# Down products of a Strassen feed-forward: operands prepared two pairs of steps ahead instead of one, with three weight tiles loaded before the loop

## The chip, the cores and the metric

The kernel runs on one core of one Trainium2 chip. The time is device microseconds (us) of one launch; the lower the better. The kernel before was timed three times: 1554.86, 1557.81 and 1557.93 us, median 1557.81.

The core's engines work in parallel, each from its own queue in program order, and wait for each other by semaphores: TensorE (PE; PEld is its weight load), VectorE (DVE), ScalarE (ACT), GpSimd (POOL) and SyncE (SP), whose queue issues the DMAs here.

## The reference

One layer of a streaming encoder over 1024 positions of 1024 channels, in float32. Its last part is what the change touches, a gated feed-forward with 2816 inner channels:

```python
h = rmsnorm(x, norm_ffn_w[l])
u = causal_dwconv(h @ w_up[l], conv_ffn_w[l]) + conv_ffn_b[l]
gate, up = jnp.split(u, 2, axis=-1)
x = x + (jax.nn.silu(gate) * up) @ w_down[l]
return rmsnorm(x, norm_final_w)
```

Before it stand an input projection, a gated delta-rule mixer, a banded attention, and an output projection. None of them is touched.

## The kernel before

**Precision.** TensorE multiplies a reduced float32 (F32R). Every operand is therefore split: a high part, made by a cast on ACT, and a low part, the operand minus its high part, made by a subtraction on DVE or POOL. A product is three matmuls: high by high, high by low, low by high.

**Down product.** `silu(gate)*up` is called y: 22 blocks of 128 inner channels. The product of y with `w_down` is done by Strassen's method with seven products of half-size matrices in place of eight. The list `plan` (line 1435) has them in the order P1, P5, P6, P3, P7, P2, P4. Each product has FH = 11 steps of 128 channels, so there are NS = 77 steps, and `down_step(s)` (line 1521) does one: 4 tiles of 128 positions times three matmuls of 128x512, that is 12 matmuls. Products accumulate in two sets of four PSUM tiles (`psd`); when a product ends, `evacuate` adds its sums to the residual `x2` on DVE, up to three a pair of steps.

**Operands of a step.** The left operand is a sum of blocks of y. These sums are formed by `a_sums` on DVE while y is made, and stored to the DRAM tensor `dA`. `a_load(k)` (line 1445) reads the two blocks of the pair k (steps 2k and 2k+1) back into a tile `araw`, of which there are two. `prep_a(k)` (line 1470) makes `ah` (ACT) and `al`: by DVE for odd k in P5, P6, P7 and P4, by POOL otherwise. There are two `ah` and two `al` tiles, the tags "hi" and "lo" of the pool `wst`, which the earlier stages use too. The right operand is a weight block of `w_down` (W11, W12, W22, W21, 11 tiles of 256 KB each) or a difference of two, which `w_sum` writes over a block, on DVE. `prep_w(k)` (line 1486) does the sums for the steps of pair k+1 and then splits the two weight blocks of pair k into `wdh` (ACT) and `wdl` (DVE). These live in five slots, `whs[s % 5]` and `wls[s % 5]`.

**Order.** Everything on DVE, ACT, POOL and SP in this stage is issued through `Pinned` (line 1162; its line 1170 is the one that the profile names), which keeps the program order on each engine. On TensorE the first matmul of each step is kept in order, and a planner places the others.

**Start of the stage.** While the last pair of up products (`r`) is still running, the pool `fr` (line 1591) takes the place of three sums of Strassen's up products, `XT1`, `XT2`, `XT3` (16 KB of high and low part a partition each), and gets W11 and the five slots. The steps 0 to 3 stand between the last pieces of the up stage: loads of W11, `prep_w(0)`, `prep_a(1)`, `prep_w(1)`, steps 0 and 1, `prep_a(2)`, `prep_w(2)`, `a_load(4)`, the last `a_sums` (four DVE operations on `yu` and two stores to `dA`), steps 2 and 3, `prep(3)`. Then the pool `fd` (line 1638) takes the place of the up stage's inputs BH and BL and of its working tiles, and gets W12, W22, W21 and `x2`.

**The loop** (line 1702) goes over the pairs k from 2. In an iteration it issues on SP `a_load(k + 2)` (from k = 3) and those loads of weights and of `x2` that are due, by a list `loads` of (step, tile, source); then `prep(k + 1)` (from k = 3, so that pair 3 is prepared ahead of the loop); then up to three evacuations, up to two steps of the final RMSNorm, and the matmuls of steps 2k and 2k+1. Steps 74 to 76 are done tile by tile after the loop, with the last sums and stores between them; pair 38 is step 76 alone, and its ah and al lie in `fr`.

Of the kernel before, what the change touches and what calls it, by code (L numbers as in the profile page):

```python
# [16 lines left out]
P = 128  # L17
# [29 lines left out]
def hybrid_kernel(ctx: ExitStack, tc: tile.TileContext, a):  # L47
# [1326 lines left out]
    def a_stores(y0, y1, i):  # L1374
        Q.dma_start(dA[0, i], y0[:, h0])
        Q.dma_start(dA[1:3, i].rearrange("s p t -> p s t"), y1.rearrange("p (s t) -> p s t", s=2))
# [65 lines left out]
    def w_src(name, f):  # L1442
        r, c = {"W11": (f, 0), "W12": (f, 1), "W22": (FH + f, 1), "W21": (FH + f, 0)}[name]
        return a["w_down"][r * P:(r + 1) * P, c * HN:(c + 1) * HN]

    def a_load(k):
        raw = wst.tile([P, 2, HN], F32, tag="raw", name="araw")
        for j in range(min(2, NS - 2 * k)):
            pi, f = divmod(2 * k + j, FH)
            Q.dma_start(raw[:, j], dA[plan[pi][1], f])  # L1450
        ring[k] = raw
# [3 lines left out]
    def w_block(s):  # L1455
        q, f = plan[s // FH][0], s % FH
        return {"P1": W11, "P3": W22, "P7": W22, "P2": W21}.get(q, W12)[f]
# [12 lines left out]
    def prep_a(k):  # L1470

        n = min(2, NS - 2 * k)
        raw = ring.pop(k)
        if n == 2:
            ah = wst.tile([P, 2, HN], F32R, tag="hi", name="ah")
            al = wst.tile([P, 2, HN], F32R, tag="lo", name="al")
        else:
            ah = fr.tile([P, 1, HN], F32R, tag="W11_0", name="ah")
            al = fr.tile([P, 1, HN], F32R, tag="W11_1", name="al")
        S.copy(ah[:, 0:n], raw[:, 0:n])  # L1480
        (V if k % 2 and plan[2 * k // FH][0] in ("P5", "P6", "P7", "P4") else G).tensor_tensor(
            out=al[:, 0:n], in0=raw[:, 0:n], in1=ah.bitcast(F32)[:, 0:n], op=ALU.subtract)
        for j in range(n):
            opa[2 * k + j] = (ah, al, j)

    def prep_w(k):

        n = min(2, NS - 2 * k)
        for s in range(2 * k + 2, min(2 * k + 4, NS)):
            if plan[s // FH][0] == "P2":  # L1490
                w_sum(s + FH)
            elif plan[s // FH][0] != "P4":
                w_sum(s)
        for s in range(2 * k, 2 * k + n):
            S.copy(whs[s % 5], w_block(s))
        for s in range(2 * k, 2 * k + n):
            V.tensor_tensor(out=wls[s % 5], in0=w_block(s), in1=whs[s % 5].bitcast(F32), op=ALU.subtract)
            opw[s] = (whs[s % 5], wls[s % 5])

    def prep(k):  # L1500

# [19 lines left out]
    def down_step(s):  # L1521
        pi, f = divmod(s, FH)
        q, ai, ac, first, dest = plan[pi]
        if f == 0 and first:
            acc[ac] = [ps_tile("psd") for _ in range(4)]
        for t in range(4):
            i = down_mm(acc[ac][t], s, t, first and f == 0, f == FH - 1 or (q == "P4" and f == FH - 4),
                        skip_group_check=not first)
            if t == 0:
                tc.keep_in_program_order(i)  # L1530
        if f == FH - 1:
            evac.extend((i, th_, dh, acc[ac][i]) for th_, dh in dest for i in range(4))
# [60 lines left out]
    def fr_tiles(name, dt, r):  # L1593
        return [fr.tile([P, HN], dt, tag=f"{name}{i}", name=f"{name}{i}") for i in r]

    W11 = fr_tiles("W11_", F32, range(5))
    for i in (0, 2):
        whs += fr_tiles("wdh", F32R, range(i, i + 2))
# [6 lines left out]
    a_load(2)  # L1605
    for f in range(5, FH):
        Q.dma_start(W11[f], w_src("W11", f))
    prep_w(0)
    r.sum_pd()
    r.P3()  # L1610
# [12 lines left out]
    p.up_b()  # L1623
    p.mul()
    a_stores(ys[0], p.yu, FH - 1)
    down_step(0)
    down_step(1)
    prep_a(2)
# [7 lines left out]
    fx.close()  # L1636
    bigx.close()
    fd = ctx.enter_context(tc.tile_pool(name="fd", bufs=1, reuse_waits="tile"))
    W12.extend(fd.tile([P, HN], F32, name=f"W12_{f}") for f in range(FH))
    x2 = [fd.tile([P, D], F32, name=f"x2_{t}") for t in range(NT)]  # L1640
    W22.extend(fd.tile([P, HN], F32, name=f"W22_{f}") for f in range(FH))
    W21.extend(fd.tile([P, HN], F32, name=f"W21_{f}") for f in range(FH))
# [2 lines left out]

    loads = []
    for f in range(FH):
        loads.append((3 + f, W12[f], w_src("W12", f)))
        loads.append((15 + f, W22[f], w_src("W22", f)))
        loads.append((34 + f, W21[f], w_src("W21", f)))  # L1650
    for b, s in (((0, 0), 6), ((1, 1), 16), ((0, 1), 27), ((1, 0), 45)):
        for i in range(4):
            t, c = 4 * b[0] + i, slice(b[1] * HN, (b[1] + 1) * HN)
# [47 lines left out]
    TAIL = NS - 3  # L1701
    for k in range(2, (NS + 1) // 2):
        s = 2 * k
        if k > 2 and 2 * (k + 2) < NS:
            a_load(k + 2)
        while loads and loads[0][0] <= s + 1:
            _, d_, s_ = loads.pop(0)
            Q.dma_start(d_, s_)
        if k > 2 and s + 2 < NS - 1:
            prep(k + 1)  # L1710
        if s + 4 == NS - 1:
            prep(k + 2)
        for _ in range(min(3, len(evac))):
            evacuate(*evac.pop(0))
        if s == 5 * FH + 5:
            normed = early_steps()
        if s == 6 * FH:
            normed = norm_steps()
        for _ in range(2):
            next(normed, None)  # L1720
        for j in range(s, min(s + 2, TAIL)):
            down_step(j)
# [96 lines left out]
```

## Time and profile before

| | |
|---|---|
| runs | 1554.86, 1557.81, 1557.93 us |
| profiled execution | 1555.1 us, span of its instructions 1553.3 us |
| PE busy | 1518.1 us (98%), 7687 matmuls |
| PEld busy | 1245.5 us (80%) |
| DVE busy | 1091.1 us (70%) |
| ACT busy | 716.3 us (46%) |
| POOL busy | 639.3 us (41%) |
| TensorE clock granted | 0.998 |
| first matmul of the down products | 1323.3 us from the span's start |
| last one | 1544.7 us |

The span counts from the first to the last instruction; what lies around it is 1.8 us. A matmul's recorded length (0.39 us) is longer than its share of the engine, since matmuls overlap: they follow one another in some 0.22 us. So the number of matmuls in a stretch tells how well PE was fed, better than its busy time does. A row of the timeline has start, length, engine, line, operation, the tiles (out<-in), the shape, the count, and in brackets the idle time ahead of it with what ended it.

### The profile page before, as it was taken

To read this page: it belongs to the slowest core of one execution; us is meant where nothing else is said; L and a number is where in the kernel's file an instruction comes from. 1 tells how busy PE (TensorE), PEld (TensorE's weight loads), DVE (VectorE), ACT (ScalarE), POOL (GpSimd) and SP (SyncE) were. 2 spreads that over 40 slices of the span, in tenths; PEclk is the share of its full clock that TensorE was granted. 3 is DMA by queue.
4 is the path that set the end of the run, shared out by engine and by line. 5 is a ranking of instruction groups with operands and counts; after the bars stand their busy time and mean duration, and the time that the engine had idled before them with its cause. 6 is when DMAs were issued, how large, how long until landed. Compare 5 with 4: busy or idle time off the path is not lost.

```text
span 1553.3 us, 21372 instructions
## 1 busy us (share of the span) xinstructions
PE 1518.1 (98%) x7687; PEld 1245.5 (80%) x7687; DVE 1091.1 (70%) x2146; ACT 716.3 (46%) x1408; POOL 639.3 (41%) x603
## 2 busy tenths in 40 slices
PE   8999999999999999999999999999999999999997
PEld 6878787877778888887887878888888888788875
DVE  7874857948436877866564477777777777786886
ACT  7735536363225656644222255444444443433344
POOL 3633323313132111111221178877777774323253
PEclk9999999999999999999999999999999999999999
DMA  8122121212131101114553223332322333764523
GB/s 300 43 70 65 52 94 45 72 49 92 57 107 50 37 24 58 50 42 153 173 164 109 95 76 108 102 102 102 102 102 102 102 102 113 268 223 161 183 82 142
DMA packets 74506, 162.04 MB, mean 104 GB/s; under 512 B 15648, under 2 KB 16928, under 8 KB 74400
## 3 DMA queue, kind: packets, MB, share of 16 engines
q1 hardware_dynamic: 74400, 160.68, 31.3%
q8 instruction: 60, 0.98, 0.3%
q14 instruction: 46, 0.38, 0.1%
HBM read 120.55 MB, written 40.11 MB: 103 GB/s over the span
## 4 chain that ended last, share of the span: by engine, by line
PE 49%; DVE 3%; issue 2%; DMA 1%; ACT 1%; SPq 1%; POOL 0%; POOLq 0%; DVEq 0%; ACTq 0%
PE psph L52 8%; PE pb L52 7%; PE psd L52 6%; PE psout L52 5%; PE pa L52 5%; PE pc L52 5%; PE pb L1156 4%; PE psd L1511 3%; PE pa L1156 3%; PE pc L1156 2%; DVE wdl L1170 1%; DVE yu L1170 1%; PE pso L52 1%; SPq L1170 1%; DMA araw<-dA 1%
## 5 line engine op out<-in xcount | busy, mean ns | idle before, releaser
L84 POOL TENSOR_TENSOR wlo<-wraw,whi 128x256 fp32r<-128x256 f32 x196 | 157.1, 831 | 442.0 <-ACT whi L81 262.8
L52 PE MATMUL psph<-BH,whi 128*128 128x512 f32 x688 | 280.1, 407 | 8.2 <-ACT BH L225 5.5
L52 PE MATMUL psph<-BL,whi 128*128 128x512 f32 x688 | 275.3, 400 | 0.1
L52 PE MATMUL psph<-BH,wlo 128*128 128x512 f32 x688 | 274.8, 399 | 0.0
L52 PEld LDWEIGHTS psph<-BH,whi 128*128 128x128 f32 x688 | 130.4, 189 | 29.9 <-ACT BH L225 5.5
L1170 POOL TENSOR_TENSOR ol<-wraw,oh 128x512 fp32r<-128x512 f32 x110 | 150.3, 1383 | 6.6 <-ACT oh L1170 6.5
L52 PEld LDWEIGHTS psph<-BL,whi 128*128 128x128 f32 x688 | 130.4, 190 | 22.5 <-DVE BL L226 2.1
L52 PEld LDWEIGHTS psph<-BH,wlo 128*128 128x128 f32 x688 | 130.3, 189 | 22.6
L1170 POOL TENSOR_TENSOR al<-araw,ah 128x1024 fp32r<-128x1024 f32 (+1 forms) x28 | 68.9, 2461 | 145.5 <-ACT ah L1170 145.4
L52 PE MATMUL psd<-wdl,ah 128*128 128x512 f32 (+1 forms) x311 | 121.1, 389 | 5.6 <-DVE wdl L1170 5.6
L52 PE MATMUL psd<-wdh,ah 128*128 128x512 f32 (+1 forms) x311 | 119.5, 387 | 1.5 <-ACT wdh L1170 1.5
L1170 POOL TENSOR_TENSOR wraw<-wraw 128x512 f32<-128x512 f32 x86 | 119.0, 1383 | 4.9
L1511 PE MATMUL psd<-wdh,al 128*128 128x512 f32 (+1 forms) x311 | 120.4, 387 | 0.0
L1170 ACT CAST oh<-wraw 128x512 fp32r<-128x512 f32 x110 | 67.8, 620 | 103.6 <-POOL wraw L1170 103.5
L1170 DVE TENSOR_TENSOR wdl<-W,wdh 128x512 fp32r<-128x512 f32 x77 | 88.9, 1192 | 28.1 <-ACT wdh L1170 28.1
L1170 ACT CAST ah<-araw 128x1024 fp32r<-128x1024 f32 (+1 forms) x39 | 40.6, 1040 | 112.9 <-PE psd L52 50.2
L81 ACT CAST whi<-wraw 128x1024 fp32r<-128x1024 f32 (+2 forms) x61 | 55.3, 907 | 79.3 <-PE psph L52 65.9
L1170 POOL TENSOR_TENSOR gl<-wraw,gh 128x512 fp32r<-128x512 f32 x42 | 56.1, 1337 | 68.9 <-ACT gh L1170 68.9
L52 PEld LDWEIGHTS psd<-wdl,ah 128*128 128x128 f32 x311 | 58.4, 188 | 19.9 <-DVE wdl L1170 8.2
L52 PEld LDWEIGHTS psd<-wdh,ah 128*128 128x128 f32 x311 | 58.4, 188 | 14.0 <-ACT wdh L1170 2.0
L1156 PE MATMUL pa<-BH,gh 128*128 128x512 f32 x176 | 68.6, 389 | 0.0
L52 PE MATMUL pa<-BH,gl 128*128 128x512 f32 x176 | 68.5, 389 | 0.0
(343 smaller groups left out, 3820.4 us busy)
## 6 DMA issues: line engine op xcount, KB each, us to landing
wraw<-w_up SPq DMA_DIRECT2D x44, 512.0 KB, 5.1
wraw<-w_tiles SPq DMA_DIRECT2D x42, 512.0 KB, 3.6
araw<-dA SPq DMA_DIRECT2D x77, 256.0 KB, 3.0
dA<-yu SPq DMA_DIRECT2D x33, 512.0 KB, 3.2
W<-w_down SPq DMA_DIRECT2D x44, 256.0 KB, 4.9
xt<-x SPq DMA_DIRECT2D x16, 512.0 KB, 5.0
dG<-gt SPq DMA_DIRECT2D x16, 512.0 KB, 2.8
ta<-dG SPq DMA_DIRECT2D x16, 256.0 KB, 3.1
```

Of the source, the lines that this page charges most:

```text
L52: last["mm"] = nc.tensor.matmul(*args, **kw).ins
L81: nc.scalar.copy(hi, src)
L84: nc.gpsimd.tensor_tensor(out=lo[:, k:k + 2], in0=src[:, k:k + 2], in1=hi.bitcast(F32)[:, k:k + 2], op=ALU.subtract)
L1156: i = nc.tensor.matmul(ps, wh[:, k], xh[:, k], start=start and k == 0, stop=False, **kw)
L1170: return lambda *args, **kw: tc.keep_in_program_order(f(*args, **kw))
L1511: i = nc.tensor.matmul(ps, al[:, j, ts], wh[:, es], start=False, stop=stop, **kw)
```

## The change

The operands of pair k+2, not of k+1, are prepared in iteration k. For that:

- a third set of `ah` and `al` in the two tiles "gt" of the pool `stg` (they held the gates of the up stage), for every k with k % 3 == 2;
- seven slots for `wdh` and `wdl` instead of five, the new ones in the tiles "p1" and "q" of the up stage;
- the first three W12 tiles in `fr`, ahead of W11, so at the place of XT1, with W11 and the slots moved up by three tiles; they are loaded on SP behind W11, ahead of `prep_w(0)`;
- the loads in the list come earlier: W12 by four steps, W22 and W21 by two;
- `a_load(k + 3)` stands where `a_load(k + 2)` stood, and `a_load(5)` is in the iteration k = 2, behind the loads that are due there (W12 tiles 3 to 6);
- `prep(k + 2)` from k = 2 on, so `prep(4)` follows `prep(3)` directly.

```diff
@@ prep_a
-            ah = wst.tile([P, 2, HN], F32R, tag="hi", name="ah")
-            al = wst.tile([P, 2, HN], F32R, tag="lo", name="al")
+            ah, al = (stg.tile([P, 2, HN], F32R, tag="gt", name=n_) if k % 3 == 2 else
+                      wst.tile([P, 2, HN], F32R, tag=t_, name=n_) for t_, n_ in (("hi", "ah"), ("lo", "al")))
@@ prep_w
-            S.copy(whs[s % 5], w_block(s))
+            S.copy(whs[s % 7], w_block(s))
...
-            V.tensor_tensor(out=wls[s % 5], in0=w_block(s), in1=whs[s % 5].bitcast(F32), op=ALU.subtract)
-            opw[s] = (whs[s % 5], wls[s % 5])
+            V.tensor_tensor(out=wls[s % 7], in0=w_block(s), in1=whs[s % 7].bitcast(F32), op=ALU.subtract)
+            opw[s] = (whs[s % 7], wls[s % 7])
@@ start of the stage
+    W12 += fr_tiles("W12_", F32, range(3))
     W11 = fr_tiles("W11_", F32, range(5))
...
     for f in range(5, FH):
         Q.dma_start(W11[f], w_src("W11", f))
+    for f in range(3):
+        Q.dma_start(W12[f], w_src("W12", f))
     prep_w(0)
...
     a_stores(ys[0], p.yu, FH - 1)
+    for t_ in ("p1", "q"):
+        whs.append(stp.tile([P, HN], F32R, tag=t_, name="wdh", bufs=2))
+        wls.append(stp.tile([P, HN], F32R, tag=t_, name="wdl", bufs=2))
     down_step(0)
...
-    W12.extend(fd.tile([P, HN], F32, name=f"W12_{f}") for f in range(FH))
+    W12.extend(fd.tile([P, HN], F32, name=f"W12_{f}") for f in range(3, FH))
...
-        loads.append((3 + f, W12[f], w_src("W12", f)))
-        loads.append((15 + f, W22[f], w_src("W22", f)))
-        loads.append((34 + f, W21[f], w_src("W21", f)))
+        if f > 2:
+            loads.append((f - 1, W12[f], w_src("W12", f)))
+        loads.append((13 + f, W22[f], w_src("W22", f)))
+        loads.append((32 + f, W21[f], w_src("W21", f)))
@@ the loop over pairs
-        if k > 2 and 2 * (k + 2) < NS:
-            a_load(k + 2)
+        if k > 2 and 2 * (k + 3) < NS:
+            a_load(k + 3)
         while loads and loads[0][0] <= s + 1:
             _, d_, s_ = loads.pop(0)
             Q.dma_start(d_, s_)
-        if k > 2 and s + 2 < NS - 1:
-            prep(k + 1)
-        if s + 4 == NS - 1:
+        if k == 2:
+            a_load(5)
+        if 2 * (k + 2) < NS:
             prep(k + 2)
```

## The prediction

> **What bounds the kernel now.** I read busy time in equal stretches first, then every wait of TensorE's weight loads (PEld) in the stage of the down products, then the other engines around those waits.
>
> ```profile
> 1320.00:1340.00 20.00, 20.00 (x90) 16.55 (x89) 14.99 (x26) 10.75 (x16) 6.73 (x3) 1.00 0.70 244
> 1340.00:1360.00 20.00, 17.86 (x77) 13.81 (x76) 15.76 (x16) 6.27 (x9) 8.00 (x4) 1.00 0.85 296
> ...
> 1400.00:1420.00 20.00, 20.00 (x90) 16.53 (x90) 12.34 (x11) 8.19 (x12) 7.20 (x3) 1.00 0.41 130
> ...
> 1480.00:1500.00 20.00, 18.29 (x81) 14.82 (x81) 18.89 (x20) 9.71 (x16) 11.66 (x6) 1.00 0.33 107
> 1500.00:1520.00 20.00, 20.00 (x89) 16.41 (x90) 14.80 (x15) 9.52 (x17) 7.98 (x5) 1.00 0.25 79
> 1520.00:1540.00 20.00, 16.74 (x72) 13.01 (x71) 15.93 (x19) 8.23 (x14) 7.79 (x5) 1.00 0.40 144
> ```
>
> The columns are: stretch, length, then PE, PEld, DVE, ACT, POOL busy with counts, granted clock, DMA share, GB/s. PE sets the pace (20.00 of 20 in most stretches), at full clock (1.00). A full stretch has 90 matmuls in 20 us, 0.222 us each. Short of 90 are 13 in 1340 to 1360, 9 in 1480 to 1500, 1 in 1500 to 1520 and 18 in 1520 to 1540: 41 matmuls, 9.1 us. That is all that better feeding of PE can give here: 2.9 us early, 6.2 us late (28 matmuls). The waits behind it:
>
> ```profile
> 1343.88 0.19 PEld L52 LDWEIGHTS psd<-wdl,ah 128*128 128x128 f32 x1 [0.85 <-DVE wdl L1170]
> 1346.67 0.19 PEld L52 LDWEIGHTS psd<-wdl,ah 128*128 128x128 f32 x1 [0.88 <-DVE wdl L1170]
> 1356.38 0.19 PEld L52 LDWEIGHTS psd<-wdl,ah 128*128 128x128 f32 x1 [1.67 <-DVE wdl L1170]
> 1499.84 0.19 PEld L52 LDWEIGHTS psd<-wdl,ah 128*128 128x128 f32 x1 [2.14 <-DVE wdl L1170]
> 1528.24 0.19 PEld L52 LDWEIGHTS psd<-wdl,ah 128*128 128x128 f32 x1 [1.27 <-DVE wdl L1170]
> 1536.65 0.19 PEld L52 LDWEIGHTS psd<-wdh,ah 128*128 128x128 f32 x1 [1.96 <-ACT wdh L1170]
> 1538.02 0.19 PEld L52 LDWEIGHTS psd<-wdl,ah 128*128 128x128 f32 x1 [1.19 <-DVE wdl L1170]
> ```
>
> Counting 24 matmuls a pair from the first down product, these are steps 6 and 7 (pair 3), 10 (pair 5), 62 (pair 31), 72 (pair 36) and 76 (pair 38). PE always waits for the split of a weight block, never for the activations.
>
> **The steady rhythm, and what the lead changes.**
>
> ```profile
> 1443.35 1.05 ACT L1170 CAST ah<-araw 128x1024 fp32r<-128x1024 f32 x1 [3.35 <-issue]
> 1448.79 1.05 ACT L1170 CAST ah<-araw 128x1024 fp32r<-128x1024 f32 x1 [3.35 <-PE psd L52]
> 1487.78 3.48 DVE L1170 TENSOR_TENSOR W<-W,W 128x512 f32<-128x512 f32 x2
> 1491.18 1.28 DVE L1170 TENSOR_TENSOR wdl<-W,wdh 128x512 fp32r<-128x512 f32 x2
> 1492.39 1.88 DVE L1170 TENSOR_TENSOR x<-psd,x 128x512 f32<-128x512 f32 x3
> 1494.18 3.92 DVE L1170 TENSOR_TENSOR W<-W,W 128x512 f32<-128x512 f32 x2
> 1498.03 4.55 DVE L1170 TENSOR_TENSOR wdl<-W,wdh 128x512 fp32r<-128x512 f32 x2
> ```
>
> A pair lasts 1448.79 - 1443.35 = 5.44 us. The split ah(k+1) starts when pair k-1 leaves its tile, so a preparation has one pair, 5.44 us, to finish. With three ah/al sets and seven wdh/wdl slots, ah(k+2) waits for the same pair k-1, at the same moment, but is due one pair later: 10.9 us. The raw ring stays at two, and a load k+3 is released by the preparation of k+1 as a load k+2 was by k. So in the steady state no engine gets work or waits added; two products just stand ready.
>
> DVE shows why the lead matters: at 1487.78 a pair needs 3.48 + 1.28 + 1.88 = 6.6 us of DVE against 5.44. Two plain subtractions take 1.28; they take 3.48 with one al on POOL beside them, 2.2 us of waiting, and 4.55 where POOL has more in a row.
>
> **Late waits, one by one.** Steps 62, 63: DVE is behind by the two W sums at 1494.18 and the locked wdl; 2.1 us late against a new slack of 5.44. The W sums of an iteration also move one iteration ahead of the ot products that POOL makes there. Removed. Step 72 is 1.3 us late behind norm work on DVE: removed. Step 76:
>
> ```profile
> 1523.70 2.06 SPq L1170 DMA_DIRECT2D out_dram<-ot  x2
> 1525.87 1.20 SPq L1170 DMA_DIRECT2D araw<-dA  x2
> 1530.08 2.07 SPq L1170 DMA_DIRECT2D out_dram<-ot  x2
> 1532.25 0.37 SPq L1170 DMA_DIRECT2D araw<-dA  x1
> 1535.46 0.62 ACT L1170 CAST ah<-araw 128x512 fp32r<-128x512 f32 x1 [3.45 <-DMA araw<-dA]
> ```
>
> The last load (1532.25) stands on SP behind the stores of ot at 1530.08, and lands at 1535.46. Moved one iteration up it stands behind the stores of 1523.70, that is at about 1525.9, 6.4 us earlier. Both waits of step 76 (1536.65 and 1538.02) go. Late gain: 6.2 us. Bounds: 0 if the lead is eaten up on the way, 6.2 if not. I take 6.2, since even the stretch with DVE at 18.89 is surrounded by 12.34 and 14.80 of 20.
>
> **The early waits** are the real question, because the lead has to be built there.
>
> ```profile
> 1333.29 1.14 ACT L1170 CAST wdh<-W 128x512 fp32r<-128x512 f32 x2
> 1336.96 1.05 ACT L1170 CAST ah<-araw 128x1024 fp32r<-128x1024 f32 x1 [2.52 <-issue]
> 1352.26 1.05 ACT L1170 CAST ah<-araw 128x1024 fp32r<-128x1024 f32 x1 [7.77 <-DMA araw<-dA]
> 1333.47 2.42 POOL L1170 TENSOR_TENSOR al<-araw,ah 128x1024 fp32r<-128x1024 f32 x1 [5.27 <-ACT ah L1170]
> 1338.09 2.40 POOL L1170 TENSOR_TENSOR al<-araw,ah 128x1024 fp32r<-128x1024 f32 x1 [2.20 <-ACT ah L1170]
> 1343.53 2.55 POOL L1170 TENSOR_TENSOR al<-araw,ah 128x1024 fp32r<-128x1024 f32 x1 [3.04 <-ACT ah L1170]
> 1335.77 1.28 DVE L1170 TENSOR_TENSOR wdl<-W,wdh 128x512 fp32r<-128x512 f32 x2
> 1339.02 4.20 DVE L1170 TENSOR_TENSOR yu<-yu 128x512 f32<-128x512 f32 x4 [1.97 <-DMA dA<-yu]
> 1343.14 3.48 DVE L1170 TENSOR_TENSOR wdl<-W,wdh 128x512 fp32r<-128x512 f32 x2
> 1353.86 3.07 DVE L1170 TENSOR_TENSOR wdl<-W,wdh 128x512 fp32r<-128x512 f32 x2 [2.19 <-ACT wdh L1170]
> 1336.34 1.28 SPq L1170 DMA_DIRECT2D araw<-dA  x2
> 1342.52 1.10 SPq L1170 DMA_DIRECT2D dA<-yu  x2
> 1343.71 2.33 SPq L1170 DMA_DIRECT2D W<-w_down  x3
> 1346.61 0.43 SPq L1170 DMA_DIRECT2D araw<-dA  x1
> DMA to landing us min/median/max: 2.6/4.0/5.6
> ```
>
> *Step 6.* ah(3) need no longer wait until 1336.96; it follows the wdh casts, at 1334.4. So al(3) follows al(2) on POOL at about 1336.5 (the first wdl of 1335.77 goes between) to 1338.9, and holds up wdl(5) to 1339.6, just when step 5 needs it. The four sums yu then start at 1339.6 and are not held up (before, the first was, by al(3) at 1338.09). At 0.73 us each, the first three end at 1341.8. But now al(4) comes early too: araw(4), issued by 1337.6, lands 2.6 to 4.0 us on, 1340.2 to 1341.6; from the start of ah to POOL's al are 1.1 us (1336.96 to 1338.09), and POOL holds the port for 2.4 us ahead of the last yu sum or of wdl(6). wdl(6) is ready at about 1345.3, not 1343.8, and wdl(7) at 1346.0, not 1346.6. The two waits become one of about 2.2; pair 3 ends about 0.6 us later than before.
>
> *Step 10.* Before, ah(5) waits for araw(5), which lands at 1352.26, 5.65 us after its second half was issued (1346.61); then al(5) holds POOL and wdl(10) is done only at 1356.4, 4.1 us after the landing. W12_0 was not what ended that wait. The diff puts a load 5 behind four tiles of W12 (3 to 6) instead of three: one more issue, 2.33 / 3 = 0.78 us. The stores before them follow the yu sums: the last one ends at 1342.5 if al(4) comes after it, at 1344.7 if before. Store 0.6, four tiles 3.1, half of araw 0.5, landing 5.65: 1352.3 or 1354.5. wdl(10) is then ready at 1356.4 or 1358.6, against 1356.38 before: 0 to 2.2 us worse, centre 1.0. Because ah(6) now follows at once, al(6) lands between wdl(10) and wdl(11): step 11 waits another 0.3.
>
> The Trainium skill, "DMA: Bandwidth & Descriptors", section "Anatomy of one DMA — SWDGE (gpsimd) path", fits 2.0 us plus bytes at 436 GB/s (for POOL's queue, not SP's): an estimate of 2.6 us for 256 KB. By it araw(5) would land about 3 us sooner, step 10 would hardly wait, and the sum would be near -7; the 5.65 us of this very load decides against it.
>
> The three early loads of W12 cost SP 3 x 0.78 = 2.3 us, in the gap before it may load araw(3); they and the moved W22 and W21 issues (two steps earlier, same count) cost nothing while PE needs none of these for 5 us; uncovered, 0.8 us a tile. The third ah/al set in the gate's tiles and the two slots in the p1 and q tiles cost nothing: their last readers, the last pair's gate and its sum with p1, stand on DVE ahead of the wdl of 1335.77. At worst a cast waits for one of them, 0.7 us as a yu sum.
>
> The 0.6 us of pair 3 goes into the wait of step 10, whose end is set by the load. New early loss: 1.0 + 0.3 = 1.3 us, between -2.9 (all waits go) and +3.5 (2.2, and 1.3 where wdl(11) too meets a whole al of 2.4).
>
> **Sum:** -6.2 + 1.3 = -4.9 us. The profiled execution took 1555.1 us (span 1553.3), the runs 1554.86, 1557.81 and 1557.93: from the profile 1550.2, from the median 1552.9. I give 1552.0, between them. The likeliest case's own range is 1549 to 1554.5.
>
> **Rivals.**
> A, *the lead is whole from the start*: araw(5) lands by about 1350, or al(4) never stands before wdl(6). All 41 matmuls come back: -9.1, from the profile 1546.0, from the median 1548.7. For it: step 10's sum for W12_0 no longer needs a load of that stretch. Against: araw(5) is queued later, not earlier.
> B, *the early stall doubles*: araw(5) lands at about 1356 or later. Early loss +3.5, net -2.7: 1552.4 to 1555.1. For it: DMA is at 0.85 in that stretch. Against: the bytes of three tiles left it.
> C, *slower*: DVE never gets ahead. If the port lock makes a pair cost DVE more than 5.44 us on average from pair 10 to 35, the lead stays nil, the late 6.2 returns, and the early 1.3 to 3.5 is paid: 1556.4 to 1558.6 against 1555.1; past 0.2% from an early loss of 3.1. For it: 6.6 us a pair at 1487.78. Against: 12.34 of 20 in 1400 to 1420.
>
> The Trainium skill, "SBUF — State Buffer", section "Who interferes with whom", says that issue order decides who is blocked, for the whole instruction. It speaks against preparing early: POOL's al issued sooner gets ahead of DVE. The 3.48 us for two wdl at 1343.14 agrees; by it alone the early loss nears case B, by DVE's turn between two POOL instructions (1498.03) it stays near 1.3.
>
> **How the numbers follow.** Forecast 0.55, A 0.17, B 0.13, C 0.15. A measurement of this kernel can tell about 0.2%, 3.1 us, from no change. Forecast and A are faster: 0.72. B and half of C are the same: 0.20. Slower: 0.08. The range 1547 to 1557 leaves out the far ends of A and C.
>
> **What would show it.** Right: no wait of PEld after 1360 on wdl or wdh; the ah casts of the steady state still 5.44 us apart; one wait near 1345 and one near 1357; 90 matmuls in each stretch from 1480 to 1540. Wrong: araw(5) landing before 1350 (A), the wait at step 62 still there (C), or a new wait on W or al in the middle, which I have not priced.

## The result, and the profile after

The changed kernel takes 1549.04 us (median of 6 runs, 1547.27 to 1550.08) against 1556.75 us for the kernel before on the same chip (median of 6): 7.7 us less, ratio 0.9948, 95% interval 0.9938 to 0.9958. The prediction was 1552.0 us with a range of 1547 to 1557. Direction and range were right; the forecast gain of 4.9 us was 2.8 us short.

The profiled execution of the changed kernel took 1549.47 us (span 1547.7). Its stage of down products began 1.65 us later than in the profile of before. Such differences come without the change too: a kernel below that is edited only near the end of the stage ("last load early") began it at 1325.00. So times of two traces are best compared from the stage's first matmul. These are the first and the last matmul of the stage, from the timeline of PE (start, duration, engine, line, operation); first before, then after.

```profile
1323.32 0.39 PE L52 MATMUL psd<-wdh,ah 128*128 128x512 f32 x1
1544.71 0.28 PE L1511 MATMUL psd<-wdh,al 128*128 128x256 f32 x1
```

```profile
1324.97 0.39 PE L52 MATMUL psd<-wdh,ah 128*128 128x512 f32 x1
1539.13 0.28 PE L1511 MATMUL psd<-wdh,al 128*128 128x256 f32 x1
```

The stage took 1544.71 - 1323.32 = 221.4 us before and 1539.13 - 1324.97 = 214.2 us after: 7.2 us less. Busy time in the same equal stretches as in the prediction (PE, PEld, DVE, ACT, POOL with counts, granted clock, DMA share, GB/s), of the changed kernel:

```profile
1340.00:1360.00 20.00, 18.62 (x81) 14.81 (x80) 15.56 (x15) 6.36 (x10) 8.21 (x4) 1.00 0.82 275
...
1480.00:1500.00 20.00, 20.00 (x90) 16.57 (x89) 18.89 (x21) 9.26 (x16) 11.19 (x7) 1.00 0.33 107
1500.00:1520.00 20.00, 20.00 (x90) 16.57 (x89) 14.63 (x14) 11.31 (x20) 9.26 (x5) 1.00 0.27 79
```

The late stretches are full: 90 matmuls where 81 stood. From 1520 to the end PE waits nowhere either. The early stretch has 81 instead of 77. All waits of TensorE's weight loads that are left in the stage:

```profile
1356.90 0.19 PEld L52 LDWEIGHTS psd<-wdl,ah 128*128 128x128 f32 x1 [1.34 <-DVE wdl L1170]
1359.69 0.19 PEld L52 LDWEIGHTS psd<-wdl,ah 128*128 128x128 f32 x1 [0.89 <-DVE wdl L1170]
```

They are steps 10 and 11. The wait near 1345 that the prediction named at step 6 is not there. The other engines around that place, in the changed kernel (start, duration, engine; in brackets the idle time before and what ended it):

```profile
1336.01 1.06 ACT L1170 CAST ah<-araw 128x1024 fp32r<-128x1024 f32 x1
1344.01 1.05 ACT L1170 CAST ah<-araw 128x1024 fp32r<-128x1024 f32 x1 [5.91 <-PE psd L52]
1352.77 1.05 ACT L1170 CAST ah<-araw 128x1024 fp32r<-128x1024 f32 x1 [6.66 <-DMA araw<-dA]
...
1340.85 2.86 DVE L1170 TENSOR_TENSOR yu<-yu 128x512 f32<-128x512 f32 x4
1343.63 1.29 DVE L1170 TENSOR_TENSOR wdl<-W,wdh 128x512 fp32r<-128x512 f32 x2
1354.37 5.27 DVE L1170 TENSOR_TENSOR wdl<-W,wdh 128x512 fp32r<-128x512 f32 x2 [4.24 <-ACT wdh L1170]
...
1335.15 5.23 POOL L1170 TENSOR_TENSOR al<-araw,ah 128x1024 fp32r<-128x1024 f32 x2 [5.28 <-ACT ah L1170]
1345.15 2.63 POOL L1170 TENSOR_TENSOR al<-araw,ah 128x1024 fp32r<-128x1024 f32 x1 [4.77 <-ACT ah L1170]
1353.89 5.20 POOL L1170 TENSOR_TENSOR al<-araw,ah 128x1024 fp32r<-128x1024 f32 x2 [6.12 <-ACT ah L1170]
...
1338.02 1.29 SPq L1170 DMA_DIRECT2D araw<-dA  x2
1343.01 1.10 SPq L1170 DMA_DIRECT2D dA<-yu  x2
1344.20 2.92 SPq L1170 DMA_DIRECT2D W<-w_down  x4
1347.22 1.81 SPq L1170 DMA_DIRECT2D araw<-dA  x4
```

ah(3) came early, at 1336.01, as the prediction said, and al(3) ran behind al(2) (POOL 1335.15, two instructions). But ah(4) came only at 1344.01, so POOL was free from 1340.4 to 1345.15. The four sums yu ran unhindered in 2.86 us (4.20 before), and wdl(6) and wdl(7) took 1.29 us from 1343.63 (3.48 before). That clears steps 6 and 7. At step 10 the picture is the predicted one: ah(5) waits for its load, al(5) and al(6) follow each other on POOL, and the two wdl beside them take 5.27 us.

### The profile page after: what moved, and what is told of

It reads as the page before. It is cut to its first block, busy times and chain, and to the rows that moved or that the text cites. A ratio compares the mean times of both kernels' runs of the same rounds, so it can differ in the third digit from the quotient of the medians.

```text
span 1547.7 us, 21371 instructions
## 1 busy us (share of the span) xinstructions
PE 1517.9 (98%) x7687; PEld 1245.4 (80%) x7687; DVE 1091.1 (70%) x2146; ACT 716.4 (46%) x1408; POOL 640.8 (41%) x603
## 3 DMA queue, kind: packets, MB, share of 16 engines
q1 hardware_dynamic: 74400, 160.68, 31.4%
## 4 chain that ended last, share of the span: by engine, by line
PE 54%; DVE 1%; DMA 1%; issue 0%; ACT 0%; POOL 0%; POOLq 0%; SPq 0%; DVEq 0%; ACTq 0%
PE psd L52 9%; PE psph L52 8%; PE pb L52 8%; PE pa L52 5%; PE psout L52 5%; PE pc L52 5%; PE psd L1511 4%; PE pb L1156 4%; PE pa L1156 3%; PE pc L1156 3%; PE pso L52 1%; PE pst L1044 0%; PE psp L877 0%; DMA tb<-dG 0%; DMA woraw<-w_out 0%
## 5 line engine op out<-in xcount | busy, mean ns | idle before, releaser
L1170 DVE TENSOR_TENSOR wdl<-W,wdh 128x512 fp32r<-128x512 f32 x77 | 95.0, 1272 | 27.6 <-ACT wdh L1170 27.5
L52 PE MATMUL pa<-BL,gh 128*128 128x512 f32 x176 | 68.5, 389 | 0.0
```

The costliest lines, as they stand in the source:

```text
L52: last["mm"] = nc.tensor.matmul(*args, **kw).ins
L1170: return lambda *args, **kw: tc.keep_in_program_order(f(*args, **kw))
```

## The experiments

Eleven kernels were made from the changed one or from the kernel before. Each was timed in five rounds or more beside the kernel before. "Against before" is the difference of the medians of one call. The stage length is worked out from the profile as above.

| kernel | against before, us | ratio, 95% interval | stage, us |
|---|---|---|---|
| before | | | 221.4 |
| changed | -7.7 | 0.9948 (0.9938 to 0.9958) | 214.2 |
| early tiles alone | -0.7 | 0.9996 (0.9987 to 1.0005) | 221.5 |
| lead alone | -5.0 | 0.9963 (0.9950 to 0.9977) | 218.4 |
| araw(5) first | -11.0 | 0.9933 (0.9920 to 0.9945) | 212.2 |
| lead from pair 12 | -9.3 | 0.9943 (0.9931 to 0.9956) | 214.2 |
| last load early | -3.6 | 0.9979 (0.9970 to 0.9988) | 218.7 |
| al(6) on DVE | -8.4 | 0.9942 (0.9928 to 0.9955) | 213.8 |
| araw(4) early | -5.9 | 0.9961 (0.9949 to 0.9973) | 216.2 |
| activations ahead | +1.4 | 1.0007 (0.9998 to 1.0016) | 223.8 |
| activations ahead, late only | -7.3 | 0.9956 (0.9942 to 0.9969) | 217.0 |
| weights ahead | -10.6 | 0.9933 (0.9921 to 0.9946) | 212.6 |
| weights ahead, two sets | -3.7 | 0.9978 (0.9968 to 0.9988) | 218.9 |

**The two parts of the change alone.** The kernel before with the three early W12 tiles and nothing else:

```diff
+    W12 += fr_tiles("W12_", F32, range(3))
...
+    for f in range(3):
+        Q.dma_start(W12[f], w_src("W12", f))
...
-        loads.append((3 + f, W12[f], w_src("W12", f)))
+        if f > 2:
+            loads.append((3 + f, W12[f], w_src("W12", f)))
```

> The kernel before with only the three early W12 tiles; no lead. My theory (the place of araw(5) in the SP queue sets the wait at step 10): araw(5) now stands behind the two stores alone, 3 x 0.78 = 2.3 us earlier, so it lands near 1350 instead of 1352.3 and wdl(10) is done near 1354, before step 10 needs it. The wait of 1.67 at step 10 goes, about 1.4 us; the waits at steps 6 and 7 and the 6.2 us of late waits stay. Total 1.4 us faster than before (0.1%). Rival (the tiles themselves were what PE waited for): the same gain, but araw(5) lands no earlier and the wait of ah(5) on its DMA is as long as before, 7.8 us. Rival (the tiles were hidden anyway): 0.

And the changed kernel without them, all W12 tiles loaded in the loop:

```diff
-    W12 += fr_tiles("W12_", F32, range(3))
...
-    for f in range(3):
-        Q.dma_start(W12[f], w_src("W12", f))
...
-        if f > 2:
-            loads.append((f - 1, W12[f], w_src("W12", f)))
+        loads.append((f - 1, W12[f], w_src("W12", f)))
```

> The changed kernel without the three early tiles: all W12 is loaded in the loop, so seven tiles instead of four stand ahead of araw(5). My theory: the late waits stay away (no wait of PEld after 1370), but araw(5) lands 3 x 0.73 = 2.2 us later than in the changed kernel, so the waits at steps 10 and 11 grow from 2.0 to about 4 us: 5 us faster than before, 2 us slower than the changed kernel. Rival (early tiles do nothing, the lead does all): as fast as the changed kernel, 7 to 8 us faster than before.

The lead alone gave 5.0 us, as expected. The early tiles alone gave nothing that can be told from zero (-0.7 us, interval -2.0 to +0.8), though their trace shows the effect that they should have: no wait at step 10, where before had one of 1.67 us, and 83 matmuls instead of 77 in 1340 to 1360. There ah(5) starts 26.0 us after the stage's first matmul instead of 28.9, so it was the place of the load, not the tiles themselves, that PE had waited for. The stage is no shorter because that trace loses the same time at its end to a lower granted clock. The last section comes back to this: the trace of the lead alone has such a place too.

**araw(5) ahead of the tiles.** The changed kernel with its load 5 issued before the four tiles of W12 instead of behind them:

```diff
     for k in range(2, (NS + 1) // 2):
         s = 2 * k
+        if k == 2:
+            a_load(5)
         if k > 2 and 2 * (k + 3) < NS:
             a_load(k + 3)
         while loads and loads[0][0] <= s + 1:
...
-        if k == 2:
-            a_load(5)
```

> The changed kernel with a_load(5) ahead of the four W12 tiles of the iteration k = 2. My theory: araw(5) is issued 2.9 us earlier and lands near 1350 instead of 1352.7, so wdl(10) is ready near 1354, when pair 4 ends (1354.9): the wait of 1.34 at step 10 goes. al(6) then runs early too and the 0.89 at step 11 goes or shrinks. 1.3 to 2.0 us faster than the changed kernel, 9 us faster than before, nearly 90 matmuls in every stretch up to 1530. Rival (the landing is set by the DMA engines' load in this stretch, not by the place in the queue): araw(5) lands within 1 us of before and the waits stay.

SP's queue and ACT of this kernel, then its early stretch:

```profile
1342.49 1.78 SPq L1170 DMA_DIRECT2D araw<-dA  x2
1344.32 1.94 SPq L1170 DMA_DIRECT2D W<-w_down  x4
...
1347.34 1.06 ACT L1170 CAST ah<-araw 128x1024 fp32r<-128x1024 f32 x1 [3.48 <-DMA araw<-dA]
```

```profile
1340.00:1360.00 20.00, 20.00 (x90) 16.57 (x89) 17.16 (x18) 8.37 (x12) 7.29 (x3) 1.00 0.92 313
```

ah(5) comes at 1347.34, that is 24.2 us after the stage's first matmul (1323.15 here) against 27.8 in the changed kernel: 3.6 us sooner, 2.0 of them because the load was issued sooner and 1.6 because it landed faster. PE has no wait left anywhere in the stage: 90 matmuls in the early stretch, the stage at 212.2 us. At 11.0 us below before it has the largest gain of this study; "weights ahead" below, with 10.6, cannot be told from it. What was left of the loss in the changed kernel was the place of one load in SP's queue, as step 10 of the prediction said.

**Where the lead matters.** The changed kernel with before's order at the start of the loop (one pair ahead, all W12 tiles loaded in the loop at before's times), and the lead of two pairs only from pair 12 on:

```diff
-    W12 += fr_tiles("W12_", F32, range(3))
...
-    for f in range(3):
-        Q.dma_start(W12[f], w_src("W12", f))
...
-        if f > 2:
-            loads.append((f - 1, W12[f], w_src("W12", f)))
+        loads.append((3 + f, W12[f], w_src("W12", f)))
...
+    LEAD = 12
     for k in range(2, (NS + 1) // 2):
         s = 2 * k
-        if k > 2 and 2 * (k + 3) < NS:
+        if k > LEAD and 2 * (k + 3) < NS:
             a_load(k + 3)
+        elif 2 < k <= LEAD:
+            a_load(k + 2)
...
-        if k == 2:
-            a_load(5)
+        if 2 < k <= LEAD:
+            prep(k + 1)
+        if k == LEAD:
+            a_load(k + 3)
-        if 2 * (k + 2) < NS:
+        if k >= LEAD and 2 * (k + 2) < NS:
             prep(k + 2)
```

> The start as in the kernel before (one pair ahead, W12 loaded in the loop), and the lead of two pairs only from pair 12 on. My theory (the late waits are lack of lead, worth 6.2 us): all waits at steps 62 to 76 go, the waits at steps 6, 7 and 10 are as before: 6.2 us faster than before, and 41 - 28 = 13 matmuls missing, all before 1360. Rival (the late gain needs the early start, or comes from another cause, such as the loads' new dates): a late wait of over 1 us stays.

All late waits are gone here too, and the stage is as long as in the changed kernel. More than expected came back, because the waits at steps 6 and 7 are missing although the loop prepares only one pair ahead there. This kernel keeps the third set of ah and al; that ah(3) no longer waits for the end of pair 1, whose tile it shares when there are two sets, was my reading of it, and the last run below shows it. (The expectation of that run says pair 0; but in before ah(3) starts at 1336.96, just behind pair 1's last matmul at 1336.71.) Two waits of 0.50 and 1.44 us are left at the start.

**The last load (step 76).** The kernel before, with the load of pair 38 issued at pair 34 into a tile of its own:

```diff
-        raw = wst.tile([P, 2, HN], F32, tag="raw", name="araw")
+        raw = (fr.tile([P, 1, HN], F32, tag="W11_2", name="araw") if 2 * k == NS - 1 else
+               wst.tile([P, 2, HN], F32, tag="raw", name="araw"))
...
-        if k > 2 and 2 * (k + 2) < NS:
+        if k > 2 and 2 * (k + 2) < NS - 1:
             a_load(k + 2)
+        if k == 34:
+            a_load(NS // 2)
```

> The kernel before with one edit: the last, half-size activation load (pair 38) is issued at pair 34 into a place of its own, instead of at pair 36 behind the stores of the norm; nothing is prepared earlier otherwise. My theory (step 76 of the prediction: the load stood on SP behind the stores of ot): both waits of step 76 go (1.96 for wdh, 1.19 for wdl), the waits at steps 62 and 72 stay as they were (2.14 and 1.27). Of the 28 matmuls short in the late stretches some 12 come back, 12 x 0.222 = 2.7 us: 2.7 us faster than before. Rival (DVE, not the load, sets step 76): the wdl wait of about 1.2 stays, at most 1.7 us faster.

The late waits of PEld in this kernel:

```profile
1500.84 0.19 PEld L52 LDWEIGHTS psd<-wdl,ah 128*128 128x128 f32 x1 [2.12 <-DVE wdl L1170]
...
1529.25 0.19 PEld L52 LDWEIGHTS psd<-wdl,ah 128*128 128x128 f32 x1 [1.28 <-DVE wdl L1170]
...
1535.68 0.19 PEld L52 LDWEIGHTS psd<-wdl,ah 128*128 128x128 f32 x1 [1.09 <-DVE wdl L1170]
```

The rival is right about the waits: the one for wdh (1.96 us) went, the one for wdl (1.19) stayed at 1.09. The place of the load behind the stores explains one of the two waits of step 76, not both. The time fell by more than either expectation, 3.6 us. Of it, 0.7 us is the wait of step 10, which was 0.94 here and 1.67 in the profile of before without an edit near it; another part seems to be the clock (last section).

**Step 11.** The changed kernel with al(6) made on DVE:

```diff
-        (V if k % 2 and plan[2 * k // FH][0] in ("P5", "P6", "P7", "P4") else G).tensor_tensor(
+        (V if k == 6 or k % 2 and plan[2 * k // FH][0] in ("P5", "P6", "P7", "P4") else G).tensor_tensor(
```

> The changed kernel with the low part al of pair 6 made on DVE, behind wdl(10) and wdl(11), instead of on POOL. My theory (step 10 of the prediction: al(6) on POOL takes the port between wdl(10) and wdl(11)): the wait of step 11 (0.89 us) goes, the wait of step 10 (1.34 us) stays, since that one hangs on the landing of araw(5); 0.6 to 0.9 us faster than the changed kernel, about 8.3 to 8.6 faster than before. Rival (step 11 waits for the late landing too, through ACT's casts): both waits stay, no gain over the changed kernel.

The PEld waits of this kernel, all that it has:

```profile
1355.63 0.76 PEld L52 LDWEIGHTS psd<-wdh,ah 128*128 128x128 f32 x4 [0.19 <-ACT wdh L1170]
1358.13 0.19 PEld L52 LDWEIGHTS psd<-wdl,ah 128*128 128x128 f32 x1 [1.74 <-DVE wdl L1170]
```

Step 11's wait is gone, and the two wdl take 3.07 us instead of 5.27: the second al on POOL was its cause. Step 10 waits 0.19 and 1.74 us here instead of 1.34; ah(5) started 28.2 us after the stage's first matmul, 0.4 us later than in the changed kernel. The net is -0.7 us against the changed kernel through the differences from before, too little to be told from zero by these intervals; the waits show the mechanism, the time does not.

**Why step 6 did not wait.** The changed kernel with araw(4) loaded into a place of its own ahead of araw(3), and prepared right behind pair 3:

```diff
-        raw = wst.tile([P, 2, HN], F32, tag="raw", name="araw")
+        raw = (fw if k == 4 else wst).tile([P, 2, HN], F32, tag="raw2" if k == 4 else "raw", name="araw", bufs=2)
...
     prep_a(1)
+    a_load(4)
     a_load(3)
...
     prep_w(2)
-    a_load(4)
...
     prep(3)
+    prep(4)
...
-        if 2 * (k + 2) < NS:
+        if k > 2 and 2 * (k + 2) < NS:
             prep(k + 2)
```

> The changed kernel with araw(4) loaded early (into a place of its own, ahead of araw(3)) and its preparation right behind that of pair 3, so that its landing no longer holds ah(4). Theory 1 (the prediction's step 6 failed only because araw(4) landed at 1344 instead of 1341): now ah(4) comes when pair 1 ends, near 1339, al(4) takes the port ahead of the yu sums and wdl(6); step 6 waits about 2 us, the stores of yu and araw(5) come later, and the kernel is 2 to 3.5 us slower than the changed one. Theory 2 (al(4) would not have got ahead of DVE anyway, since DVE takes its turn): no wait at step 6, and the time is that of the changed kernel within 1 us, or up to 1 us faster since a load less stands ahead of araw(5).

ACT, POOL, DVE and PEld of this kernel:

```profile
1338.24 1.05 ACT L1170 CAST ah<-araw 128x1024 fp32r<-128x1024 f32 x1 [0.52 <-issue]
1354.48 1.05 ACT L1170 CAST ah<-araw 128x1024 fp32r<-128x1024 f32 x1 [14.14 <-DMA araw<-dA]
...
1334.34 8.04 POOL L1170 TENSOR_TENSOR al<-araw,ah 128x1024 fp32r<-128x1024 f32 x3 [5.27 <-ACT ah L1170]
...
1340.05 5.07 DVE L1170 TENSOR_TENSOR yu<-yu 128x512 f32<-128x512 f32 x4
...
1345.77 0.19 PEld L52 LDWEIGHTS psd<-wdl,ah 128*128 128x128 f32 x1 [1.46 <-DVE wdl L1170]
1356.10 0.76 PEld L52 LDWEIGHTS psd<-wdh,ah 128*128 128x128 f32 x4 [0.48 <-ACT wdh L1170]
1358.59 0.19 PEld L52 LDWEIGHTS psd<-wdl,ah 128*128 128x128 f32 x1 [1.73 <-DVE wdl L1170]
```

Theory 1 holds. With the data there in time, ah(4) comes at 1338.24, three al run in a row on POOL to 1342.4, the sums yu take 5.07 us instead of 2.86, and step 6 waits 1.46 us. Step 11 waits 0.88 us, as in the changed kernel. The stores of yu and araw(5) behind them come later: counted from the stage's first matmul (1324.63 here), ah(5) starts after 29.9 us instead of 27.8. The stage is 2.0 us longer than in the changed kernel. So the chain that the prediction described at step 6 is real; the changed kernel escaped it only because araw(4) landed late. The Trainium skill, "SBUF — State Buffer", section "Who interferes with whom", which the prediction weighed, says that issue order decides who blocks for the whole instruction. The 5.07 us on DVE beside POOL's 8.04 agree with a lock, but not with one that POOL keeps from one al to the next: in the same stretch DVE finished two wdl, from 1336.63 to 1340.13.

**Which operand has to be ahead.** The changed kernel, in the loop only the activations two pairs ahead, the weight splits one:

```diff
         if 2 * (k + 2) < NS:
-            prep(k + 2)
+            prep_a(k + 2)
+        if k > 2 and 2 * (k + 1) < NS:
+            prep_w(k + 1)
```

> The changed kernel, but in the loop only the activations are prepared two pairs ahead; the weight splits stay one pair ahead, as before the change. My theory (TensorE waited for the split of a weight block, never for the activations; at step 76 the split was late because its cast stood on ACT behind a late ah): the waits at steps 62, 63 and 72 stay (2.14, 0.20, 1.27), those of step 76 go. 16 of the 28 late matmuls stay lost, 16 x 0.222 = 3.6 us: 3.6 us slower than the changed kernel. Rival (the early al alone frees DVE, since POOL no longer locks it beside the wdl that is due): the late waits go as well, and the time is that of the changed kernel.

The start spoiled this run. These are PEld and ACT near the first wait:

```profile
1353.18 0.19 PEld L52 LDWEIGHTS psd<-wdh,ah 128*128 128x128 f32 x1 [5.02 <-ACT wdh L1170]
...
1351.57 1.04 ACT L1170 CAST ah<-araw 128x1024 fp32r<-128x1024 f32 x1 [7.53 <-DMA araw<-dA]
1352.52 1.14 ACT L1170 CAST wdh<-W 128x512 fp32r<-128x512 f32 x2
```

wdh(8), due for step 8, now stands on ACT behind ah(5), which waits for its load until 1351.57. That queueing I had not seen when I wrote the expectation; it costs 5.02 us, 2.28 us more at wdl(8), and a stretch of half clock behind them (last section), and the time is no better than before's. Its late waits, 2.13 us at step 62 and 0.22 at step 72, were those expected. To see them without that start, the edit was made again from pair 14 on only, with the changed kernel's loop ahead of it:

```diff
         if 2 * (k + 2) < NS:
-            prep(k + 2)
+            prep_a(k + 2)
+            if k < 12:
+                prep_w(k + 2)
+        if k > 12 and 2 * (k + 1) < NS:
+            prep_w(k + 1)
```

> The changed kernel up to pair 14; from there on only the activations are prepared two pairs ahead, and the weight splits one. It is the run on the activations' lead without its start, where the split of step 8 stood on ACT behind the cast of the late araw(5) and cost a wait of 5.02 us. My theory: no wait of 5 us at the start, only the 1.34 and 0.89 us of the changed kernel; the wait at step 62 comes back with about 2.1 us and one of 0.2 to 1.3 at step 72; none at step 76. 2.3 to 3.5 us slower than the changed kernel. Rival (that run's wait at step 62 came from its shifted start): no late wait, time of the changed kernel.

Its late waits:

```profile
1499.03 0.19 PEld L52 LDWEIGHTS psd<-wdl,ah 128*128 128x128 f32 x1 [2.14 <-DVE wdl L1170]
...
1526.33 0.19 PEld L52 LDWEIGHTS psd<-wdl,ah 128*128 128x128 f32 x1 [0.22 <-DVE wdl L1170]
```

The waits are as expected: that of step 62 is back in full, that of step 72 as 0.22, none at step 76, and the stage is 2.9 us longer than in the changed kernel (0.3 us of that is step 10, which waits 1.62 here). The time does not confirm the loss: by the medians it is only 0.4 us (-7.3 against -7.7), with intervals of some 3 us, and the stage lengths come from one profile each.

The other half: the weight splits two pairs ahead, the activations one.

```diff
-        if k > 2 and 2 * (k + 3) < NS:
-            a_load(k + 3)
+        if k > 2 and 2 * (k + 2) < NS:
+            a_load(k + 2)
...
-        if k == 2:
-            a_load(5)
+        if k > 2 and 2 * (k + 1) < NS:
+            prep_a(k + 1)
         if 2 * (k + 2) < NS:
-            prep(k + 2)
+            prep_w(k + 2)
```

> The changed kernel, but in the loop only the weight splits are prepared two pairs ahead; the activations stay one pair ahead and their loads two, as before the change. My theory (TensorE waited for weight splits): the waits at steps 62, 63 and 72 are gone as in the changed kernel. At step 76 the cast ah(38) waits for its load behind the stores of the norm again, but the weight split of step 76 stands ahead of it on ACT: so the wait there moves from the split to the activation, or goes; it is 0 to 2 us. Start: araw(5) as in the changed kernel. In all 0 to 2 us slower than the changed kernel, at least 5.5 faster than before. Rival (the early al was what freed DVE): the wait of about 2.1 us at step 62 comes back, and the kernel is 3 us or more slower than the changed one.

```profile
1354.75 0.30 PEld L1511 LDWEIGHTS psd<-wdh,al 128*128 128x128 f32 x2 [0.62 <-POOL al L1170]
...
1348.38 1.28 DVE L1170 TENSOR_TENSOR wdl<-W,wdh 128x512 fp32r<-128x512 f32 x2
...
1351.17 1.05 ACT L1170 CAST ah<-araw 128x1024 fp32r<-128x1024 f32 x1 [4.39 <-DMA araw<-dA]
```

The first line, from PEld, is the only wait of the stage, 0.62 us. No late wait came back, nor one at step 76, and the kernel is 10.6 us below before, better than I expected; its stage of 212.6 us is 1.6 shorter than the changed kernel's. The reason is in the other two lines: ah(5) lands as late as ever, at 1351.17, but wdl(10) is ready by 1349.7, ahead of it. In the changed kernel one preparation makes ah(5) and then wdh(10), so the wait for wdl at step 10 is the wait for araw(5) in disguise, with the split and its time on DVE still to follow.

In that kernel the third set of ah and al still lets an activation be prepared before the pair ahead of it has left its tile. Without that set:

```diff
-            ah, al = (stg.tile([P, 2, HN], F32R, tag="gt", name=n_) if k % 3 == 2 else
-                      wst.tile([P, 2, HN], F32R, tag=t_, name=n_) for t_, n_ in (("hi", "ah"), ("lo", "al")))
+            ah = wst.tile([P, 2, HN], F32R, tag="hi", name="ah")
+            al = wst.tile([P, 2, HN], F32R, tag="lo", name="al")
```

> The kernel with only the weight splits two pairs ahead, and without the third set of ah/al (two sets, as before the change). My theory: late, two sets are enough, since the activations are again prepared one pair ahead: no wait after 1360. At the start, ah(3) must wait for the end of pair 0 again, al(3) falls beside the yu sums and wdl(6), and the waits at steps 6 and 7 come back (0.85 and 0.88 us): 1 to 2 us slower than the kernel with three sets and the weight lead, 8.5 to 9.5 us faster than before. Rival (steps 6 and 7 were cured by something else in the edit, such as the early tiles or the order of the loads): no wait at steps 6 and 7, 10.5 us faster than before.

```profile
1344.53 0.19 PEld L52 LDWEIGHTS psd<-wdl,ah 128*128 128x128 f32 x1 [0.86 <-DVE wdl L1170]
1347.32 0.19 PEld L52 LDWEIGHTS psd<-wdl,ah 128*128 128x128 f32 x1 [0.89 <-DVE wdl L1170]
...
1533.46 0.19 PEld L52 LDWEIGHTS psd<-wdh,ah 128*128 128x128 f32 x1 [2.16 <-ACT ah L1170]
1534.81 0.29 PEld L1511 LDWEIGHTS psd<-wdh,al 128*128 128x128 f32 x1 [1.06 <-POOL al L1170]
```

The waits of steps 6 and 7 are back as expected, so it is the third set that cures them. My "no wait after 1360" was wrong: step 62 stays cured, but step 72 waits 0.51 us for al, and step 76 now waits 2.16 us for ah and 1.06 for al, with 3.4 us of half clock behind it (last section). The gain shrinks to 3.7 us. Two sets are not enough at the end, where the last load is late: it is issued 205.7 us after the stage's first matmul here and 198.9 with three sets, from the same place in SP's order.

## Why the prediction was right, and where it was not

**Late term, -6.2 us: right.** PE's late stretches are full, the waits of steps 62, 63, 72 and 76 are all gone, and the casts of ah in the steady state still stand 5.44 us apart (1438.52 and 1443.96). The runs also say which part does it. At step 62 it is the weight splits' lead: with the activations alone ahead the 2.14 us come back in full. At step 72 the activations' lead alone already takes 1.27 us down to 0.22, and the weight splits' lead leaves no wait for wdl. Step 76 is clear with the third set, whichever operand leads; with two sets the earlier load alone leaves 1.09 us, and the weight splits' lead alone 2.16 and 1.06. "PE always waits for the split of a weight block, never for the activations" holds as a reading of the kernel before; for steps 10 and 76 it named the last instruction of a chain that began with the load of an activation. At step 76 the prediction had the right end for half a reason: the load's place on SP explains the wait for wdh, not that for wdl.

**Early term, +1.3 us: wrong in sign.** Before, 13 matmuls were missing in 1340 to 1360; the prediction added 1.3 us to their 2.9, which makes 4.2. Missing are 90 - 81 = 9, that is 2.0 us: -0.9 instead of +1.3. The step that failed is *Step 6*, "But now al(4) comes early too", with araw(4) landing at 1340.2 to 1341.6. Its row of landing times ran from 2.6 to 5.6 us; I took the lower half, although *Step 10*, a paragraph later, used 5.65 us for a load of the same kind. ah(4) came at 1344.01, 4.7 us after its second half was issued (1338.02 + 1.29 = 1339.31). The run with araw(4) loaded early did what step 6 described, 1.46 us of wait where 2.2 were forecast, and lost 2.0 us of stage against the changed kernel. The trace names PE as what ended ACT's idle time before ah(4); in four of the variants (araw(5) first, lead alone, lead from pair 12, al(6) on DVE) the same cast, after 5.6 to 6.1 us of idle time, is put down to the load. It follows the end of the load's issue by 4.5 to 4.9 us in these four and by 4.7 in the changed kernel. So the landing set it there, and most likely here, where pair 2 happened to end at the same time (its last matmul starts at 1343.80).

**Step 10** took over that error. Its centre of 1.0 us was the middle between "last sum yu ahead of al(4)" and "behind it", and only the first came true. Counted from the stage's first matmul, the loads of araw(5) were issued at 1347.22 - 1324.97 = 22.3 us, and ah(5) started after 27.8 us; before, after 1352.26 - 1323.32 = 28.9. The fourth tile did stand ahead of the load, at 2.92 / 4 = 0.73 us, but the stores came 1.2 us sooner since the sums were not held up. PE, freed of the waits at steps 6 and 7, reached step 10 sooner too, after 29.9 us instead of 31.4, so a wait stayed. It is 0.3 us shorter than before's 1.67, where 1.0 more was forecast. The waits that remain are where the prediction put them, at step 10 (1.34 us) and step 11 (0.89 us, forecast "another 0.3"); al(6) between wdl(10) and wdl(11) is confirmed as the cause of the second.

**The rivals.** A's condition was "araw(5) lands by about 1350, or al(4) never stands before wdl(6)". The second half came true, but step 10 still waited, so only part of its gain came. B and C did not occur. By its size, -7.2 us of stage lies about halfway between forecast (-4.9) and A (-9.1). Of the 2.3 us by which the stage beat the forecast, 2.2 are the early term. That the time still fell into the range owes something to its width: 1549.04 us is the very end of the likeliest case's own range, 1549 to 1554.5.

**What stood in no step:** the granted clock after a stall, below. The profile that the sum started from (1555.1 us, clock 0.998) has no dip of it in this stage, but 24 of the 62 later runs of before have that clock too, and their mean is 1556.6 us. So the clock alone does not explain why that profile lay under the median of before.

## What to carry to other kernels

When operands of two kinds are prepared in one go, look which of them hangs on a late load: a cast that is ready to run but stands behind it on the same queue inherits its delay, and the wait then shows under the wrong name. Giving only the weight splits the longer lead came out at 10.6 us here and giving it to both at 7.7 (stages of 212.6 and 214.2 us; the intervals of the two ratios just overlap). Moving one load of activations ahead of four tiles of W12, with both ahead, gave 11.0 us. In a blind sum, use one landing time for all loads of one stretch, or carry both ends of it through every step that hangs on it.

## What the runs showed of the hardware

**After a group of stalls the granted clock can halve for 3.4 or 6.8 us.** The run of activations ahead, in stretches of 2 us behind its wait of 5.02 us (columns as above; the granted clock is the third number from the end):

```profile
1352.00:1354.00 2.00, 0.64 (x1) 0.19 (x1) 0.83 (x1) 2.00 (x4) 1.31 (x1) 0.85 1.00 373
...
1356.00:1358.00 2.00, 2.00 (x6) 1.52 (x6) 2.00 (x1) 0.00 (x0) 1.82 (x1) 0.50 0.98 296
1358.00:1360.00 2.00, 2.00 (x6) 1.60 (x5) 2.00 (x4) 0.00 (x0) 0.00 (x0) 0.50 1.02 247
```

Six matmuls in 2 us instead of ten or eleven. It happens after shorter waits too. The run of the lead alone has two, of 1.95 and 1.71 us, with four matmuls between them:

```profile
1356.00:1358.00 2.00, 1.13 (x4) 0.59 (x4) 2.00 (x1) 2.00 (x4) 2.00 (x2) 0.91 0.59 216
1358.00:1360.00 2.00, 1.60 (x4) 1.31 (x5) 2.00 (x2) 0.37 (x1) 2.00 (x1) 0.50 0.59 160
1360.00:1362.00 2.00, 2.00 (x7) 1.52 (x6) 2.00 (x3) 0.71 (x1) 0.57 (x1) 0.50 1.03 253
1362.00:1364.00 2.00, 2.00 (x6) 1.62 (x5) 2.00 (x4) 1.37 (x3) 0.00 (x0) 0.50 0.83 280
1364.00:1366.00 2.00, 2.00 (x9) 1.60 (x9) 2.00 (x4) 0.00 (x0) 0.00 (x0) 0.89 1.03 361
```

The three middle rows are at half speed throughout, the first and the last for 0.36 and 0.44 us of their 2: 6.8 us in all, as in the run of activations ahead. It cost some 2.8 us of the stage (218.4 - 214.2 us, less the 1.4 us by which the waits are longer than in the changed kernel). The early tiles alone had 3.4 us of it behind the two waits of step 76 (1.98 and 1.19 us), and the weights ahead with two sets 3.4 us behind 2.16 and 1.06. The profile of before behind the same two waits of step 76 (1.96 and 1.19) had none, nor had the changed kernel behind 1.34 and 0.89 us, nor the run with araw(4) early behind 0.48, 1.73 and 0.88. The Trainium skill, "TensorE: Matmul & The Clock Gate", section "Part 1: The HAM clock gate", has a free-running window of about 3.4 us and a fall to half speed after an idle one. The half speed agrees (0.50), and so do the lengths, one such window or two. So does the chance in it: behind the same two waits one profile has the dip and another has not. That four matmuls in the middle of the idle time do not prevent it is more than the rule says.

It also bears on the result. Over 62 timed runs of before beside the experiments the mean granted clock was 0.9972, over the 6 of the changed kernel 0.9982, over the 11 with the last load early 0.9984. The four kernels whose profile shows a dip have 0.9955 to 0.9968, the six others 0.9982 to 0.9984. A thousandth of 1555 us is 1.6 us. So part of what the removal of step 76's double wait gained, about 1 to 2 us in the median, seems to be clock and not waiting time. That this accounts for the whole difference between stage and median was not tested.

**A landing is not one number.** SP and ACT of the changed kernel at the last load of activations:

```profile
1524.41 0.37 SPq L1170 DMA_DIRECT2D araw<-dA  x1
...
1527.52 0.62 ACT L1170 CAST ah<-araw 128x512 fp32r<-128x512 f32 x1 [3.34 <-DMA araw<-dA]
```

Loads of 256 KB from the same place through the same queue took, from the end of the issue to the cast that waited, 2.7 us here (1527.52 - 1524.78), 4.7 us for araw(4) and, with 1.81 / 4 = 0.45 us an issue, 4.6 us for araw(5) (1352.77 - 1348.13). The DMA engines were busy to 0.82 there and to 0.30 in the last stretch of the stage (1520 to 1540). Their load is not all of it: issued ahead of the four tiles of W12 instead of behind them, araw(5) took 3.1 us (1347.34 - 1344.27) in a stretch where they were busy to 0.92. The last load is also a single one, the others the second of two; which of these counts was not tested.
